# Forming the weights of two neighbouring outputs at once in the second pass of a gated MLP

## The chip, the cores and the metric

The kernel runs on one core of a Trainium2 chip. It is one program that computes the whole network below. The metric is the device time of one execution in microseconds (us); the shown number is the median of several executions. A core has five engines that run their own instruction streams side by side: TensorE (PE in the profile, matrix products into PSUM), VectorE (DVE) and GpSimd (POOL) for elementwise work, ScalarE (ACT) for elementwise functions, and SyncE (SP), which here issues the DMA transfers between device memory and SBUF, the on-chip memory.

## The reference, cut to what matters

Two layers, 1024 tokens of width 1024, float32. Each layer has a mixer (attention in the first, a matrix memory in the second) and then this MLP with D_FF = 2816:

```python
def conv_ffn(h, w_up, conv_w, conv_b, w_down):
    a, g = jnp.split(h @ w_up, 2, axis=-1)
    a = lax.conv_general_dilated(a, conv_w[:, None, :], ...) + conv_b
    return (jax.nn.gelu(a, approximate=False) * g) @ w_down
...
    h = rms_norm(x) * (1 + sc_f) + sh_f
    x = x + g_f * conv_ffn(h, ffn_w_up[i], ffn_conv_w[i], ffn_conv_b[i], ffn_w_down[i])
```

The change touches only the product with w_down (2816 x 1024), once in each layer.

## The kernel before, in words

Activations are held transposed: 128 features on the partitions, 512 tokens (half of the sequence) along the free dimension. Weights come in tiles of 128 input features by 128 output features.

**Three products for one.** A float32 matrix `v` is held as two: `hi`, the ScalarE copy of `v` in the format fp32r, and `lo = v - hi`, the rest, formed by a subtraction on VectorE or GpSimd. `mm3` (L172 to L177) forms one product as `hi*hi`, then `hi` of the weight with `lo` of the activation, then `lo` of the weight with `hi` of the activation. So PE needs the weight's `lo` first at the third matmul of a tile.

**Seven products for eight.** The MLP is a 2x2 block product done with seven block products instead of eight (a Strassen-Winograd scheme). In the second pass the blocks of the weight are: the output tiles p = 0..3 against p + 4 (two rows of blocks), and two halves of the input features (two columns). For one p, A11 and A12 are the blocks of output p, A21 and A22 those of output p + 4. The weights' operands of the seven products are named in the code B11 (A11), B21 (A12), T1 (the sum A21 + A22), B22, T2, T3 (derived from the sum and the blocks by three subtractions in `derive`) and T4 (A22). The 22 tiles of input features are worked on in three groups `DG` of n = 4, 4 and 3 tiles in each half. A group runs its seven products in the order `ORD`, and each product for p = 0, 1, 2, 3: 28 entries of 3n matmuls. Every entry is added to the running x by `gate_x` (L290 to L294, VectorE, reads PSUM) as soon as it is finished.

**How the weights are formed.** For each group and p, `weights` loads two tiles of 128x1024 (L1152): one with A11 and A12, asked for at B11, and one with A21 and A22, asked for at T1. `d_sum` (L1163) forms the sum of 128x512 into half of a `wsum` tile, `derive` (L1171 to L1173) forms the three differences in place, and `wop` (L988, L989) forms `hi` and `lo` into half of a pair of tiles of 128x1024, so that two entries share a pair. In the last group the width is 384 and not 512. The rest `lo` is formed on GpSimd for T3 and T4, and also for B11 and B21 in the groups after the first; on VectorE otherwise.

**The order of the work.** The list `seq` holds all entries of both passes; the loop at the end of `mlp` forms an entry's weights five entries before it runs it (`LOOK`). Hooks of that list load the activations (`q`, L1121) and x (L1222) and form the activations' operands `U` (L1138 to L1140, VectorE and ScalarE, 128x1024 each). All loads go through SP's queue in order. There are four pairs of `hi` and `lo` tiles, five tiles `raw` (A11, A12 and others), four tiles `raw1` (A21, A22) and two `wsum`. A new load waits until its slot is free. The framework arranges each engine's instructions ahead of time by program order, dependencies and its own estimates of cost, so that the order on an engine can differ from the order in the code; on the chip each engine then runs its list strictly in order. Instructions under `tc.high_priority()`, such as `gate_x`, are put ahead.

## Time and profile before

| | |
|---|---|
| median of 3 runs | 2198.36 us (2195.66 to 2200.03) |
| the profiled execution: span from first to last instruction | 2200.1 us (its time outside the span is not shown) |
| PE busy | 2166.5 us, 98% |
| DVE busy | 1693.1 us, 77% |
| ACT busy | 1046.7 us, 48% |
| POOL busy | 178.3 us, 8% |
| mean granted clock of TensorE | 0.994 |
| second pass of the first layer, first and last matmul into the banks da | start at 903.6 us and 1106.4 us |
| second pass of the second layer, last matmul into da | starts at 2188.4 us |

In the profile's rows, a line such as `x<-da,modc,x` says what an instruction writes and from what, by the names in the code: `whi` and `wlo` are a weight's hi and lo, `da` and `db` the second pass's PSUM banks, `U` its activations' operands, `raw` and `wsum` the weights before they are split. A number in brackets at the end of a timeline row is the time that the engine was idle before the instruction, and what ended it. A row with `x2` joins two instructions that follow each other, and its duration is of both together.

### The profile page before, as it was taken

The page shows a single profiled execution, that of the slowest core. Times are in us where ns is not written, and L with a number is a line of the kernel's source. Part 1 is how long each engine was busy: PE and PEld are TensorE (multiplying, and loading weights), DVE is VectorE, ACT ScalarE, POOL GpSimd, SP SyncE. Part 2 cuts the span into 40 slices and gives each one's busy share as a digit, 9 for nine tenths or more (in the row PEclk, how much of TensorE's full clock was granted, in tenths as well). Part 3 has the DMA queues.
Part 4 walks back from the last instruction along what each step waited for, and adds up shares of the span by engine and source line. Part 5 has one row for each costly group of instructions (what it writes and reads, how often), then busy time and mean ns, then how long its engine had stood idle before and what let it go on. Part 6 is the DMA issues. An engine that isn't in the chain of part 4 may idle for free.

```text
span 2200.1 us, 28740 instructions
## 1 busy us (share of the span) xinstructions
PE 2166.5 (98%) x10557; PEld 1818.0 (83%) x10557; DVE 1693.1 (77%) x2769; ACT 1046.7 (48%) x1812; POOL 178.3 (8%) x216
## 2 busy tenths in 40 slices
PE   9999999999999999999999999999999999999998
PEld 7878888787888888877888888988788888887787
DVE  8877878669878777899973655566887777778997
ACT  6465556446544444543453434344554444453335
POOL 0000000000000000042210111010000000002232
PEclk9999999999999999999999999999999999999999
DMA  8512234832444332542132243444143332245122
GB/s 317 152 50 63 92 109 142 285 125 69 157 139 143 123 125 85 204 151 89 53 121 93 62 131 103 132 157 171 64 144 101 111 120 92 79 163 194 50 80 77
DMA packets 105085, 270.50 MB, mean 123 GB/s; under 512 B 12336, under 2 KB 15984, under 8 KB 104944
## 3 DMA queue, kind: packets, MB, share of 16 engines
q1 hardware_dynamic: 104544, 268.28, 36.9%
q8 instruction: 83, 1.36, 0.3%
q14 instruction: 58, 0.48, 0.1%
q10 hardware_dynamic: 400, 0.39, 0.1%
HBM read 221.53 MB, written 44.47 MB: 121 GB/s over the span
## 4 chain that ended last, share of the span: by engine, by line
PE 85%; DVE 9%; DMA 3%; ACT 2%; issue 1%; POOL 0%; SPq 0%; POOLq 0%; DVEq 0%; ACTq 0%
PE pa L175 7%; PE pa L177 7%; PE pa L176 7%; PE pd L177 3%; PE pd L175 3%; PE pd L176 3%; PE sc L673 3%; PE op L175 3%; PE op L176 3%; PE op L177 2%; PE inp L177 2%; PE da L175 2%; PE inp L175 2%; PE inp L176 2%; PE da L176 2%; PE db L175 2%
## 5 line engine op out<-in xcount | busy, mean ns | idle before, releaser
L988 ACT ACTIVATE whi<-raw 128x512 fp32r<-128x512 f32 (+1 forms) x252 | 147.3, 607 | 243.2 <-PE pb L176 61.0
L988 ACT ACTIVATE whi<-wsum 128x512 fp32r<-128x512 f32 (+1 forms) x224 | 134.0, 617 | 181.8 <-PE pa L176 61.5
L175 PE MATMUL pa<-T,whi 128*128 128x512 f32 x528 | 205.9, 390 | 0.0
L176 PE MATMUL pa<-T,whi 128*128 128x512 f32 x528 | 205.4, 389 | 0.0
L177 PE MATMUL pa<-T,wlo 128*128 128x512 f32 x528 | 205.1, 389 | 0.0
L989 DVE TENSOR_TENSOR wlo<-wsum,whi 128x512 fp32r<-128x512 f32 (+1 forms) x224 | 151.1, 690 | 32.8 <-ACT whi L988 31.5
L989 POOL TENSOR_TENSOR wlo<-raw,whi 128x512 fp32r<-128x512 f32 (+1 forms) x80 | 119.9, 1515 | 401.7 <-ACT whi L988 394.0
L175 PE MATMUL da<-U,whi 128*128 128x512 f32 (+1 forms) x364 | 139.5, 383 | 3.4 <-DVE x L294 3.4
L177 PE MATMUL da<-U,wlo 128*128 128x512 f32 (+1 forms) x364 | 138.4, 383 | 2.0 <-DVE wlo L989 2.0
L176 PE MATMUL da<-U,whi 128*128 128x512 f32 (+1 forms) x364 | 139.2, 382 | 0.0
L989 DVE TENSOR_TENSOR wlo<-raw,whi 128x512 fp32r<-128x512 f32 (+1 forms) x172 | 115.7, 679 | 24.9 <-ACT whi L988 24.9
L167 ACT ACTIVATE whi<-wraw 128x1024 fp32r<-128x1024 f32 x67 | 70.7, 1059 | 117.1 <-PE op L176 59.2
L175 PEld LDWEIGHTS pa<-T,whi 128*128 128x128 f32 x528 | 99.1, 188 | 22.2 <-ACT whi L988 1.2
L177 PEld LDWEIGHTS pa<-T,wlo 128*128 128x128 f32 x528 | 99.1, 188 | 20.6
L176 PEld LDWEIGHTS pa<-T,whi 128*128 128x128 f32 x528 | 99.1, 188 | 20.3
L1140 DVE TENSOR_TENSOR U<-q,U 128x1024 fp32r<-128x1024 f32 x84 | 102.9, 1241 | 14.0 <-ACT U L1139 13.6
L1028 ACT ACTIVATE ct<-a,cols 128x512 f32<-128x512 f32 x88 | 70.8, 808 | 83.9 <-DVE a L1050 47.9
L175 PE MATMUL db<-U,whi 128*128 128x512 f32 x264 | 103.3, 391 | 1.3 <-ACT whi L988 1.3
L168 DVE TENSOR_TENSOR wlo<-wraw,whi 128x1024 fp32r<-128x1024 f32 x67 | 81.7, 1222 | 29.4 <-ACT whi L167 27.2
L177 PE MATMUL db<-U,wlo 128*128 128x512 f32 x264 | 102.9, 390 | 0.0
L176 PE MATMUL db<-U,whi 128*128 128x512 f32 x264 | 102.8, 389 | 0.0
L1139 ACT ACTIVATE U<-q 128x1024 fp32r<-128x1024 f32 x84 | 79.7, 979 | 47.7 <-DVE q L1138 22.2
(378 smaller groups left out, 6097.3 us busy)
## 6 DMA issues: line engine op xcount, KB each, us to landing
raw<-in_wf SPq DMA_DIRECT2D x96, 512.0 KB, 4.0
wraw<-in_w SPq DMA_DIRECT2D x67, 512.0 KB, 3.7
mraw<-in_mod_w SPq DMA_DIRECT2D x56, 512.0 KB, 4.0
ud<-ct SPq DMA_DIRECT2D x88, 256.0 KB, 2.4
q<-ud SPq DMA_DIRECT2D x88, 256.0 KB, 4.6
raw<-in_wd SPq DMA_DIRECT2D x32, 512.0 KB, 6.4
pa<-in_mod_w SPq DMA_DIRECT2D x24, 512.0 KB, 3.7
x<-xd SPq DMA_DIRECT2D x48, 256.0 KB, 4.8
```

Of the source, the lines that this page charges most:

```text
L167: act.activation(hi, raw, AF.Copy)
L168: dve.tensor_tensor(lo, raw, hi.bitcast(F32), ALU.subtract)
L175: pe.matmul(ps, lh, rh, start=first, stop=False, skip_group_check=more)
L176: pe.matmul(ps[:, 0:rl.shape[-1]], lh, rl, start=False, stop=False, skip_group_check=more)
L177: pe.matmul(ps, ll, rh, start=False, stop=last, skip_group_check=more)
L673: pe.matmul(ps[:, cs], a[:, qs if n < 3 else qrs_], b[:, cs], start=n == 0, stop=n == 4)
L988: act.activation(hi, src, AF.Copy)
L989: eng.tensor_tensor(lo, src, hi.bitcast(F32), ALU.subtract)
L1028: act.activation(t, a[:, 2:], AF.Identity, bias=col(f"cb{l}", m), scale=cw(m, 2))
L1139: act.activation(hi, w, AF.Copy)
L1140: dve.tensor_tensor(lo, w, hi.bitcast(F32), ALU.subtract)
```

## The change

Everything that `weights`, `d_sum`, `derive` and `d_w` did for one output p is now done for the outputs p and p + 1 together. A load no longer brings two blocks of one output, but one block of two outputs (`block_of`, with b = 0..3 for A11, A12, A21, A22): 512 KB as before, in two runs of 2 KB per partition where there was one of 4 KB. So A11 of a pair is asked for at B11, A12 at B21, and A21 and A22 at T1, each at the even p of the pair. The sum (`two_sum`), the three differences (`derive`) and the split into `hi` and `lo` (`d_two`) work on 128x1024 (128x768 in the last group) and are issued once for a pair, five entries ahead of the even p; the odd p's entry then finds its parts ready. The choice of engine for each rest is the same. Numbers and sizes of the tiles are the same, and so are all matmuls and everything outside the second pass.

```diff
--- before.py
+++ after.py
@@ -1144,44 +1144,56 @@
             for _ in operand(i):
                 pass
 
-        def weights(g, p, i):
+        def block_of(g, p, b):
 
             k0, n = DG[g]
-            if (g, p, i) not in W:
-                t = (pd[0] if i else px).tile([P, 1024], F32, tag=f"raw{i}" if i else "raw", bufs=4 if i else RAWS, name=nm("raw"))
-                nc.sync.dma_start(t[:, 0:2 * n * P], wd[l, p + 4 * i, :, k0 * P:(k0 + 2 * n) * P])
-                W[g, p, i] = t[:, 0:n * P], t[:, n * P:2 * n * P]
-            return W[g, p, i]
-
-        sums = []
-
-        def d_sum(g, p):
-            if not sums:
-                t = wp.tile([P, 1024], F32, tag="wraw", bufs=wraws, name=nm("wsum"))
-                sums.extend(t[:, i * HS:(i + 1) * HS] for i in range(2))
-            W[g, p, "s"] = sums.pop(0)[:, 0:DG[g][1] * P]
-            dve.tensor_tensor(W[g, p, "s"], *weights(g, p, 1), ALU.add)
+            if (g, p, b) not in W:
+                t = (pd[0] if b > 1 else px).tile([P, 1024], F32, tag="raw1" if b > 1 else "raw",
+                                                  bufs=4 if b > 1 else RAWS, name=nm("raw"))
+                c0 = (k0 + b % 2 * n) * P
+                v = t[:, 0:2 * n * P]
+                nc.sync.dma_start(v.rearrange("q (p c) -> q p c", p=2),
+                                  wd[l, p + b // 2 * 4:p + b // 2 * 4 + 2, :, c0:c0 + n * P].rearrange("p q c -> q p c"))
+                W[g, p, b] = v
+            return W[g, p, b]
+
+        def two_sum(g, p):
+
+            W[g, p, "s"] = wp.tile([P, 1024], F32, tag="wraw", bufs=wraws, name=nm("wsum"))[:, 0:2 * DG[g][1] * P]
+            dve.tensor_tensor(W[g, p, "s"], block_of(g, p, 2), block_of(g, p, 3), ALU.add)
             return W[g, p, "s"]
 
         def derive(g, p):
 
             if (g, p, "d") not in W:
                 W[g, p, "d"] = True
-                sm, (a11, a12), (a21, _) = W[g, p, "s"], weights(g, p, 0), weights(g, p, 1)
+                sm, a11, a12, a21 = W[g, p, "s"], *[block_of(g, p, b) for b in range(3)]
                 dve.tensor_tensor(sm, sm, a11, ALU.subtract)
                 dve.tensor_tensor(a11, a11, a21, ALU.subtract)
                 dve.tensor_tensor(a21, a12, sm, ALU.subtract)
 
+        def d_two(g, p, op):
+            if op in ("B11", "B21"):
+                src, eng = block_of(g, p, int(op == "B21")), pool if g else dve
+            elif op == "T1":
+                src, eng = two_sum(g, p), dve
+            elif op == "T4":
+                src, eng = block_of(g, p, 3), pool
+            else:
+                derive(g, p)
+                src = {"B22": block_of(g, p, 2), "T2": W[g, p, "s"], "T3": block_of(g, p, 0)}[op]
+                eng = pool if op == "T3" else dve
+            n = src.shape[-1]
+            hi, lo = [wp.tile([P, 1024], F32R, tag=f"w{j}", bufs=wbufs, name=nm(f"w{j}"))[:, 0:n] for j in ("hi", "lo")]
+            act.activation(hi, src, AF.Copy)
+            eng.tensor_tensor(lo, src, hi.bitcast(F32), ALU.subtract)
+            for i in range(2):
+                W[g, p + i, op] = [x[:, i * n // 2:(i + 1) * n // 2] for x in (hi, lo)]
+
         def d_w(g, p, op):
-            if op in ("B11", "B21"):
-                return wop(weights(g, p, 0)[op == "B21"], pool if g else dve)
-            if op == "T1":
-                return wop(d_sum(g, p), dve)
-            if op == "T4":
-                return wop(weights(g, p, 1)[1], pool)
-            derive(g, p)
-            return wop({"B22": weights(g, p, 1)[0], "T2": W[g, p, "s"], "T3": weights(g, p, 0)[0]}[op],
-                       pool if op == "T3" else dve)
+            if (g, p, op) not in W:
+                d_two(g, p, op)
+            return W[g, p, op]
 
         bank_a, bank_d, stats = {}, {}, {}
 
@@ -1245,11 +1257,7 @@
                         hook(len(seq) - 1, lambda i=i, gen=gen: gen.append(operand(i + 3)))
                     if p in (0, 2) and t0 == 0 and 0 < i and i + 3 < len(order):
                         hook(len(seq) - 1, lambda gen=gen, p=p: piece(gen[0], 1 + p))
-                    if t0 == 0:
-                        make = lambda g=g, p=p, op=op: W.setdefault((g, p, op), None) or W.__setitem__(
-                            (g, p, op), d_w(g, p, op)) or W[g, p, op]
-                    else:
-                        make = lambda g=g, p=p, op=op: W[g, p, op]
+                    make = lambda g=g, p=p, op=op: d_w(g, p, op)
                     seq.append((make, lambda w, i=i, p=p, t0=t0, width=width: d_run(i, p, w, t0, width)))
```

## The prediction

> **What bounds the kernel now.** I read the page's busy shares and chain first, then the engines' shares in the stages of the second pass, then TensorE's waits there one by one, and last what VectorE and GpSimd did just before each wait.
>
> ```profile
> span 2200.1 us, 28740 instructions
> PE 2166.5 (98%) x10557; PEld 1818.0 (83%) x10557; DVE 1693.1 (77%) x2769; ACT 1046.7 (48%) x1812; POOL 178.3 (8%) x216
> ...
> PE 85%; DVE 9%; DMA 3%; ACT 2%; issue 1%; POOL 0%; SPq 0%; POOLq 0%; DVEq 0%; ACTq 0%
> ```
>
> TensorE (PE) is busy for 98% of the span, and the change takes no matmul away. It can only save time in which PE waits inside the MLPs' second passes, so I look for that time. The four stretches below are the first group of each layer's second pass (919 to 960 and 1980 to 2021) and the change from its first to its second group (960 to 1000 and 2021 to 2061).
>
> ```profile
> 919.00:960.00 41.00, 39.36 (x172) 31.74 (x171) 40.42 (x54) 13.69 (x20) 2.98 (x2) 1.00 0.46 171
> 960.00:1000.00 40.00, 38.65 (x170) 31.41 (x169) 34.99 (x33) 17.78 (x25) 23.91 (x14) 1.00 0.36 128
> 1980.00:2021.00 41.00, 39.35 (x172) 31.93 (x172) 40.65 (x53) 13.94 (x21) 2.98 (x2) 1.00 0.45 164
> 2021.00:2061.00 40.00, 37.95 (x165) 30.53 (x165) 34.03 (x32) 17.45 (x24) 24.46 (x14) 1.00 0.37 128
> ```
>
> The columns are PE, weight loads, VectorE (DVE), ScalarE (ACT), GpSimd (POOL), each in us with its count, then the granted clock, the DMA share and GB/s. DVE is full in the first stretch (40.42 of 41) while ACT works a third of it; in the second, POOL works 23.91 of 40. The granted clock is 1.00 throughout. PE's waits there, all of them above 0.15 us:
>
> ```profile
> 951.79 0.50 PE L177 MATMUL da<-U,wlo 128*128 128x512 f32 x1 [1.01 <-DVE wlo L989]
> 955.45 0.50 PE L175 MATMUL db<-U,whi 128*128 128x512 f32 x1 [0.63 <-ACT whi L988]
> 994.21 0.47 PE L175 MATMUL da<-U,whi 128*128 128x512 f32 x1 [0.82 <-DVE x L294]
> 997.74 0.47 PE L175 MATMUL da<-U,whi 128*128 128x512 f32 x1 [0.53 <-DVE x L294]
> 2012.48 0.50 PE L177 MATMUL da<-U,wlo 128*128 128x512 f32 x1 [1.00 <-DVE wlo L989]
> 2016.14 0.50 PE L175 MATMUL db<-U,whi 128*128 128x512 f32 x1 [0.65 <-ACT whi L988]
> 2051.93 0.47 PE L175 MATMUL da<-U,whi 128*128 128x512 f32 x1 [0.56 <-DVE x L294]
> 2055.84 0.47 PE L175 MATMUL da<-U,whi 128*128 128x512 f32 x1 [0.95 <-DVE x L294]
> 2059.38 0.47 PE L175 MATMUL da<-U,whi 128*128 128x512 f32 x1 [0.53 <-DVE x L294]
> ```
>
> In the first layer they add up to 1.01+0.63+0.82+0.53 = 2.99 us, in the second to 1.00+0.65+0.56+0.95+0.53 = 3.69. So **6.7 us is the most that the change can gain** here. They are of two kinds: **place one**, where weights' parts (rests) come late in the first group, and **place two**, where the addition of a finished product to x (L294) comes late as the second group begins. Both are lateness of DVE.
>
> **The change part by part.** The 84 pairs of hi and lo parts of each layer's second pass become 42 pairs of double width; so do 12 sums (6) and 36 derived blocks (18). In group 0, T3 and T4 have their rests on POOL and the other five products on DVE; in groups 1 and 2 it is four on POOL and three on DVE. On DVE that is 20+12+12 rests, 12 sums and 36 derived blocks, or 92 instructions that become 46.
>
> *VectorE.* Two half-width instructions back to back against one of full width:
>
> ```profile
> 928.18 0.69 DVE L1163 TENSOR_TENSOR wsum<-raw 128x512 f32<-128x512 f32 x1 [0.57 <-DMA raw<-in_wd]
> 928.79 1.22 DVE L1138 TENSOR_TENSOR q<-q 128x1024 f32<-128x1024 f32 x1
> 929.92 0.75 DVE L294 SCALAR_TENSOR_TENSOR x<-db,modc,x 128x512 f32<-128x512 f32 x1
> 930.58 1.28 DVE L989 TENSOR_TENSOR wlo<-wsum,whi 128x512 fp32r<-128x512 f32 x2
> ```
>
> Two of 128x512 take 1.28 us together and one of 128x1024 takes 1.22, so a merged pair saves 0.06. The 46 pairs save 2.8 us of DVE a layer, but only those before a wait count. In 926.9 to 951.7 I count 22 such instructions (4 sums, 4+3+1 rests, 10 derived), 11 pairs: 0.7 us before place one, in each layer.
>
> [...]
>
> *GpSimd.* The changed kernel has a 128x1024 rest here, which this trace does not show. The nearest rows:
>
> ```profile
> 960.37 1.29 POOL L989 TENSOR_TENSOR wlo<-raw,whi 128x512 fp32r<-128x512 f32 x1 [9.18 <-ACT whi L988]
> 1055.58 1.02 POOL L989 TENSOR_TENSOR wlo<-raw,whi 128x384 fp32r<-128x384 f32 x1 [2.46 <-ACT whi L988]
> ```
>
> 128 elements more cost 0.27, so 512 cost 1.08 and 0.21 is fixed: a pair takes about 2.37 (an estimate; bounds 2.16 with no fixed part, 2.58 for two whole ones), and 0.21 is saved, within 0 to 0.42. While POOL works, DVE's two-input instructions are slowed:
>
> ```profile
> 985.57 1.66 DVE L1140 TENSOR_TENSOR U<-q,U 128x1024 fp32r<-128x1024 f32 x1
> 987.15 2.31 DVE L1138 TENSOR_TENSOR q<-q,q 128x1024 f32<-128x1024 f32 x1
> 989.38 0.74 DVE L294 SCALAR_TENSOR_TENSOR x<-da,modc,x 128x512 f32<-128x512 f32 x1
> ...
> 982.57 5.80 POOL L989 TENSOR_TENSOR wlo<-raw,whi 128x512 fp32r<-128x512 f32 x3 [2.78 <-PE da L177]
> ```
>
> 1.22 became 2.31, about one POOL instruction more (1.09 of 1.29), and POOL's three took 5.80 and not 3.87; L294, which reads PSUM, kept its 0.74. In 960 to 1000 stand 14 POOL instructions; as 7 pairs they save 7 x 0.21 = 1.5 us of POOL. I take half as given back to DVE (bounds 0 and all): 0.7 a layer, just before place two.
>
> *ScalarE.* One conversion of 128x1024 costs 1.06 for two of 0.61 to 0.62:
>
> ```profile
> L988 ACT ACTIVATE whi<-raw 128x512 fp32r<-128x512 f32 (+1 forms) x252 | 147.3, 607 | 243.2 <-PE pb L176 61.0
> L167 ACT ACTIVATE whi<-wraw 128x1024 fp32r<-128x1024 f32 x67 | 70.7, 1059 | 117.1 <-PE op L176 59.2
> L168 DVE TENSOR_TENSOR wlo<-wraw,whi 128x1024 fp32r<-128x1024 f32 x67 | 81.7, 1222 | 29.4 <-ACT whi L167 27.2
> ```
>
> ACT's own saving I cost at nothing, since ACT idles two thirds of the first stretch; without that cover it would be 42 x 0.15 = 6 us a layer.
>
> *What comes later for the first of a pair.* Its parts now wait for the second: +0.45 us on ACT, +0.54 on DVE (1.22 less 0.68), +1.08 on POOL, and its three derived blocks +1.6. The kernel forms weights five products ahead, and one product is 12 matmuls, 0.23 us apart (below), 2.7 us, so 13.6 us cover this unless DVE's backlog has eaten them, as it has at place one. There the second of the pair comes earlier by nearly as much. I take no net cost, with 0.54 a layer (the rest of T2's second output formed before its first can run) as the upper bound.
>
> *Loads.* Bytes and counts stay: four 512 KB tiles per group and half, now as 256 runs of 2 KB and not 128 of 4 KB. SP's queue is passed by them in another order: A12's blocks are asked for at B21 and no longer at B11, ahead of x's tiles of half 0.
>
> ```profile
> raw<-in_wd SPq DMA_DIRECT2D x32, 512.0 KB, 6.4
> out<-x SPq DMA_DIRECT2D x4, 512.0 KB, 2.8
> 920.53 2.79 SPq L1152 DMA_DIRECT2D raw<-in_wd x4
> 926.92 0.68 DVE L1163 TENSOR_TENSOR wsum<-raw 128x512 f32<-128x512 f32 x1
> 931.03 0.39 PE L175 MATMUL db<-U,whi 128*128 128x512 f32 x1
> 931.26 0.39 PE L176 MATMUL db<-U,whi 128*128 128x512 f32 x1
> ```
>
> The stores to out have that same split form and land in 2.8, in a quiet queue; the loads' 6.4 is queueing. I take the split as free (bounds: 2.8 and 6.4 to land). A12's block goes into a tile slot that was free before, so I expect no delay of x. But T1's **first sum now waits for two blocks**: the second one landed just before 928.18, and the sum would start then and not at 926.92. DVE idles 1.26 there in place of 0.57, so 0.7 are lost in the first layer. Behind it in DVE's order stand a difference of q, an addition to x and the rest, and PE wants that rest at 931.26+0.23 = 931.49. In the second layer the sums start late enough that the second block is nearly there:
>
> ```profile
> 1987.68 1.28 DVE L1163 TENSOR_TENSOR wsum<-raw 128x512 f32<-128x512 f32 x2
> ```
>
> There, I take 0.4 (bounds 0 and 0.7).
>
> *Sum.* Place one: 0.7 saved less 0.7 waited = 0 in the first layer, 0.7-0.4 = 0.3 in the second. Place two: 0.7 in each, and two pairs of sums there, 2 x 0.06 = 0.1 each: 1.6. Together 1.9 us, so the profiled 2200.1 would become 2198.2. This profile's span lies 1.7 above the median of the runs, 2198.36; no time outside the span is shown. From the median: 2198.36-1.9 = **2196.4**. Its own range: nothing saved at place two and 0.54 lost twice is 2198.36-0.3+1.1 = 2199.2, and everything given back (0.7 more a layer) with no wait for blocks 2198.36-1.9-1.4-1.1 = 2194.0.
>
> **The rivals.**
> *A, the waits vanish.* If the order of DVE's work also falls better, since A12's slot comes free when the blocks are derived and not at T3, and the next group's loads start earlier, all 6.7 us go: 2191.7. For it speaks that every wait is under 1.02 us; against it that place two is overload by POOL, whose elements stay.
>
> *B, POOL holds DVE longer (slower).* Place: the additions to x at the change to the second group, and T2's first rest at place one:
>
> ```profile
> 948.21 2.98 POOL L989 TENSOR_TENSOR wlo<-raw,whi 128x512 fp32r<-128x512 f32 x2 [98.17 <-ACT whi L988]
> 948.30 1.74 DVE L1171 TENSOR_TENSOR wsum<-wsum,raw 128x512 f32<-128x512 f32 x1
> 949.96 1.77 DVE L989 TENSOR_TENSOR wlo<-wsum,whi 128x512 fp32r<-128x512 f32 x1
> ```
>
> Two DVE instructions that take 0.68 elsewhere take 1.74 and 1.77 beside two of POOL, and PE's wait at 951.79 follows. If a DVE instruction is held for one whole POOL instruction, it is held 2.37 in place of 1.29, 1.08 more, with an addition to x queued behind it. At each of the seven waits of these kinds (2+5) that is +7.6: 2206.0. It decides as soon as additions to x have less than 1.08 us of room before their bank is wanted again, and at five places they have none. Against it: as many elements pass POOL, so half as many instructions are held.
>
> [...]
>
> *C, the wait for two blocks decides.* The sum starts at 928.18, ends 1.22 later at 929.4; the conversion (1.06) ends at 930.5; with the difference of q (1.13) and the addition (0.67) ahead of it, the rest runs from 931.2 to 932.4, and PE waits 0.9 at 931.49. With 0.4 in the second layer, and nothing gained: 2198.36+1.3 = 2199.7.
>
> *D, it does nothing on the path*, if DVE's order is so fixed by other work that each saved bit becomes idle time: 2198.4.
>
> **How the numbers follow.** The forecast (a gain of up to 4.4) has 0.38, A 0.25, B 0.20, C 0.12, D 0.05. A measurement of this kernel can tell 0.2%, 4.4 us, from no change. Faster than that are A and the forecast's best end (0.09): 0.34. Slower are B and the case that C meets a worse order of work (0.04): 0.24. The rest is 0.42. The range reaches to A with more gained outside the waits, 2189, and to all of B, 2206.
>
> **What would show it.** Right: 42 pairs of parts a layer, DVE's 128x1024 rests at 1.22 and POOL's near 2.4 alone; the waits at place two shorter by half a microsecond a layer, those at place one nearly as before. B shows as DVE instructions of 3.5 us and additions to x that release PE later. C shows as a wait of T1's first product for its rest, and an idle DVE of over 1 us before the first sum. The prediction is wrong if the order of products on PE changes in the second pass, or if a wait appears at B22's third product, whose derived blocks now come in one lump of 3.6 us.

## The result, and the profile after

The changed kernel takes **2211.64 us** (median of 5 runs, 2209.56 to 2212.59), the kernel before 2198.36 (5 runs, 2195.3 to 2200.86). The ratio is 1.0065, with a 95% interval of 1.0054 to 1.0075: the change costs 13.3 us. It was forecast to save 2.

The page of the changed kernel begins as follows; the last line is the chain that ended last.

```profile
span 2209.7 us, 28482 instructions
PE 2169.6 (98%) x10557; PEld 1819.9 (82%) x10557; DVE 1702.4 (77%) x2677; ACT 1037.5 (47%) x1728; POOL 159.7 (7%) x176
...
PE 83%; DVE 10%; DMA 3%; ACT 2%; issue 1%; SPq 1%; POOL 0%; DVEq 0%; POOLq 0%; ACTq 0%
```

The counts are those of the edit: VectorE (DVE) has 92 instructions fewer, ScalarE (ACT) 84 and GpSimd (POOL) 40. POOL is 18.6 us less busy and ACT 9.2. But DVE is **9.3 us busier** with fewer instructions, where 46 merged pairs a layer at 0.06 each should have made it 2 x 46 x 0.06 = 5.5 us less busy. Some 15 us of DVE's time therefore went into instructions that took longer than their work.

The same stretches as in the prediction, by engine (columns: PE, weight loads, DVE, ACT, POOL in us with counts, granted clock, DMA share, GB/s):

```profile
919.00:960.00 41.00, 39.50 (x173) 31.72 (x172) 39.38 (x38) 13.77 (x14) 7.29 (x2) 1.00 0.58 193
960.00:1000.00 40.00, 36.88 (x155) 29.59 (x154) 38.41 (x29) 15.38 (x16) 17.31 (x6) 0.96 0.25 87
1980.00:2021.00 41.00, 39.55 (x173) 31.82 (x172) 39.20 (x38) 13.25 (x13) 7.29 (x2) 1.00 0.60 195
2021.00:2061.00 40.00, 33.91 (x144) 27.01 (x143) 38.22 (x29) 15.02 (x15) 16.59 (x6) 0.98 0.30 96
```

The first stretch of each layer is as before (173 matmuls in both, before 172 in both). The second has lost 15 matmuls in the first layer and 21 in the second, and DVE is fuller there (38.41 and 38.22, before 34.99 and 34.03), with 29 instructions where there were 33 and 32. PE's waits in these places:

```profile
930.88 0.50 PE L177 MATMUL db<-U,wlo 128*128 128x512 f32 x1 [1.10 <-DVE wlo L1189]
947.45 0.50 PE L175 MATMUL db<-U,whi 128*128 128x512 f32 x1 [0.40 <-ACT whi L1188]
980.67 0.79 PE L175 MATMUL da<-U,whi 128*128 128x512 f32 x1 [2.91 <-DVE x L294]
...
1993.16 0.50 PE L177 MATMUL db<-U,wlo 128*128 128x512 f32 x1 [1.05 <-DVE wlo L1189]
2009.75 0.50 PE L175 MATMUL db<-U,whi 128*128 128x512 f32 x1 [0.40 <-ACT whi L1188]
2043.10 0.50 PE L175 MATMUL da<-U,whi 128*128 128x512 f32 x1 [3.04 <-DVE x L294]
2052.55 0.47 PE L175 MATMUL da<-U,whi 128*128 128x512 f32 x1 [0.99 <-ACT whi L1188]
2057.59 0.50 PE L175 MATMUL da<-U,whi 128*128 128x512 f32 x1 [2.06 <-DVE x L294]
...
2176.93 0.38 PE L250 MATMUL st<-ones,ssq 128*128 128x1 f32 x2 [0.47 <-DVE ssq L241]
2178.26 0.40 PE L250 MATMUL st<-ones,sq 128*128 128x1 f32 x2 [0.94 <-ACT sq L229]
```

Place one (the first two and the fourth and fifth row) makes 1.10+0.40+1.05+0.40 = 2.95, before 0.63+1.01+1.00+0.65 = 3.29. Place two, with a small further wait of 0.21 at 996.2, makes 2.91+0.21+3.04+0.99+2.06 = 9.2, before 3.4. The last two rows are new: the sums of squares for the final norm at the end.

After some of these waits TensorE runs at half clock for a while. Three windows of the changed kernel show it in the granted clock, the column behind that of POOL:

```profile
980.00:984.00 4.00, 3.33 (x8) 2.65 (x9) 4.00 (x5) 1.06 (x1) 0.00 (x0) 0.57 0.00 0
2059.00:2063.00 4.00, 4.00 (x13) 3.09 (x12) 4.00 (x5) 1.06 (x1) 0.00 (x0) 0.57 0.00 0
2176.00:2188.00 12.00, 10.59 (x43) 8.73 (x42) 5.17 (x9) 5.79 (x13) 2.82 (x2) 0.72 0.00 0
```

A clock of 0.57 over 4 us is a loss of 0.43 x 4 = 1.7 us, which is half of a stretch of 3.4 us; 0.72 over 12 us is a loss of 0.28 x 12 = 3.4, two such stretches. Together they cost 6.8 us. The kernel before had a clock of 1.00 at the same work, in the second-pass rows of the prediction and at its end:

```profile
2166.00:2178.00 12.00, 12.00 (x64) 10.18 (x64) 7.06 (x12) 8.04 (x17) 4.58 (x5) 1.00 0.00 1
```

The granted clock of the changed kernel is 0.50 from 980.41 to 983.82 us, from 2059.02 to 2062.43 and from 2178.49 to 2185.31: two stretches of 3.41 us, and one of 6.82. The last section has the rows of PE's work ahead of them.

Both kernels have 10557 matmuls in the trace, and they can be matched by number except at one place in each layer, inside the first two groups of the table below. There the order of products on PE has changed: from 950.2 us the kernel before runs 14 matmuls into da, two into db, six into da and ten into db, and the changed kernel from 948.5 us five into da and then twenty into db. T2's first product, which waited for its rest at 951.79 before, now stands mostly behind B22's. Groups that begin and end outside that place hold the same matmuls in both kernels, so the time that they take is the sharpest view of where the 13.3 us lie:

| from matmul to matmul | before | after | |
|---|---|---|---|
| 4391 to 4730 (919 to 1000 us before: first layer, group 0 and the change to group 1) | 81.1 | 84.4 | +3.3 |
| 9597 to 9932 (1980 to 2061 us: the same in the second layer) | 81.0 | 86.7 | +5.7 |
| 10368 to the last (2160 to 2193 us: the end) | 32.8 | 37.5 | +4.7 |
| sum | | | +13.7 |

Outside these three the changed kernel's execution is 4 us faster, by luck of the clock and not by the change. The code there is the same, and the half-clock stretches near 10, 116 and 1350 us last 6.8, 6.8 and 3.4 us in this execution of the kernel before, but 3.4, 3.4 and nothing in that of the changed one, which is 5.1 us of time. So the spans differ by only 9.6 us, while the medians differ by 13.3. The first 40 us of before, and then of after:

```profile
0.00:40.00 40.00, 35.57 (x146) 29.75 (x147) 31.35 (x56) 25.24 (x40) 0.77 (x8) 0.91 0.87 315
```

```profile
0.00:40.00 40.00, 36.08 (x151) 30.29 (x152) 31.25 (x56) 25.73 (x41) 0.77 (x8) 0.96 0.89 319
```

**How the long wait comes about.** VectorE and GpSimd of the changed kernel ahead of PE's wait at 980.67:

```profile
956.51 2.76 DVE L1138 TENSOR_TENSOR q<-q 128x1024 f32<-128x1024 f32 x1
969.86 3.45 DVE L1138 TENSOR_TENSOR q<-q,q 128x1024 f32<-128x1024 f32 x1
973.89 6.06 DVE L1140 TENSOR_TENSOR U<-q,U 128x1024 fp32r<-128x1024 f32 x2
979.88 0.74 DVE L294 SCALAR_TENSOR_TENSOR x<-da,modc,x 128x512 f32<-128x512 f32 x1
```

```profile
955.43 2.76 POOL L1189 TENSOR_TENSOR wlo<-raw,whi 128x1024 fp32r<-128x1024 f32 x1 [0.58 <-DMA q<-ud]
961.39 2.50 POOL L1189 TENSOR_TENSOR wlo<-raw,whi 128x1024 fp32r<-128x1024 f32 x1 [3.20 <-DMA raw<-in_wd]
969.71 2.52 POOL L1189 TENSOR_TENSOR wlo<-raw,whi 128x1024 fp32r<-128x1024 f32 x1 [5.81 <-ACT whi L1188]
```

POOL's first ends at 955.43+2.76 = 958.19. DVE's instruction from 956.51 ends at 959.27, which is 1.08 us later, close to its own 1.22: it gets to its work about when POOL has ended. The same holds at 969.86: POOL ends at 972.23, DVE at 973.31, again 1.08 later. POOL's pair takes 2.50 where it is not held itself (961.39). An instruction of 1.22 us now takes 2.76 to 3.45. The addition to x (L294) keeps its 0.74 as before, but it stands behind two such instructions (6.06 us together), ends at 980.62, and 0.05 later PE starts.

The group rows of 54 us around the change to group 1 in the first layer, of before and then of after, have ten additions to U each:

```profile
L1140 DVE TENSOR_TENSOR U<-q,U 128x1024 fp32r<-128x1024 f32 x10 | 14.9, 1501 | 2.5 <-ACT U L1139 2.5
```

```profile
L1140 DVE TENSOR_TENSOR U<-q,U 128x1024 fp32r<-128x1024 f32 x10 | 18.9, 1896 | 1.7 <-ACT U L1139 1.7
```

Ten of 1.22 would be 12.2. They are held for 2.7 us before and 6.7 after. POOL gains in the same exchange: three rests of 128x512 took 5.80 beside DVE before, so two of them 3.87, and its pair takes 2.76 now. In the second layer's 54 us the additions to U and the differences of q show the same, again before and then after:

```profile
L1140 DVE TENSOR_TENSOR U<-q,U 128x1024 fp32r<-128x1024 f32 x11 | 16.2, 1476 | 3.4 <-ACT U L1139 3.4
L1138 DVE TENSOR_TENSOR q<-q 128x1024 f32<-128x1024 f32 x4 | 4.8, 1213 | 0.0
```

```profile
L1140 DVE TENSOR_TENSOR U<-q,U 128x1024 fp32r<-128x1024 f32 x9 | 16.1, 1801 | 1.8 <-ACT U L1139 1.8
L1138 DVE TENSOR_TENSOR q<-q 128x1024 f32<-128x1024 f32 x6 | 10.4, 1754 | 0.0
```

11 x 1.22 = 13.4, so 2.8 held before; 9 x 1.22 = 11.0 and 6 x 1.22 = 7.3, so 5.1+3.1 = 8.2 after. With all groups that are held (the other differences of q, the sums and the rests too), the held time goes from 9.0 to 13.5 us in the first layer's window and from 9.0 to 14.2 in the second's: 9.7 us more.

### The profile page after: what moved, and what is told of

Read it like the earlier page. It is cut to its first block, busy times and chain, and to the rows that moved or that the text cites. A ratio compares the mean times of both kernels' runs of the same rounds, so it can differ in the third digit from the quotient of the medians.

```text
span 2209.7 us, 28482 instructions
## 1 busy us (share of the span) xinstructions
PE 2169.6 (98%) x10557; PEld 1819.9 (82%) x10557; DVE 1702.4 (77%) x2677; ACT 1037.5 (47%) x1728; POOL 159.7 (7%) x176
## 3 DMA queue, kind: packets, MB, share of 16 engines
q1 hardware_dynamic: 110688, 268.28, 37.5%
## 4 chain that ended last, share of the span: by engine, by line
PE 83%; DVE 10%; DMA 3%; ACT 2%; issue 1%; SPq 1%; POOL 0%; DVEq 0%; POOLq 0%; ACTq 0%
PE pa L175 7%; PE pa L177 7%; PE pa L176 7%; PE sc L673 3%; PE pd L177 3%; PE pd L175 3%; PE pd L176 3%; PE op L175 2%; PE op L176 2%; PE op L177 2%; PE inp L177 2%; PE inp L175 2%; PE inp L176 2%; PE db L177 2%; PE db L175 2%; PE db L176 2%
## 5 line engine op out<-in xcount | busy, mean ns | idle before, releaser
L988 ACT ACTIVATE whi<-wsum 128x512 fp32r<-128x512 f32 x176 | 107.2, 625 | 126.7 <-PE pa L176 61.5
L989 DVE TENSOR_TENSOR wlo<-wsum,whi 128x512 fp32r<-128x512 f32 x176 | 118.3, 687 | 32.5 <-ACT whi L988 31.2
L1189 POOL TENSOR_TENSOR wlo<-raw,whi 128x1024 fp32r<-128x1024 f32 (+1 forms) x40 | 99.9, 2498 | 433.6 <-DVE wlo L1189 204.3
L988 ACT ACTIVATE whi<-raw 128x512 fp32r<-128x512 f32 x132 | 79.8, 624 | 109.0 <-PE pb L176 61.0
L1140 DVE TENSOR_TENSOR U<-q,U 128x1024 fp32r<-128x1024 f32 x84 | 113.9, 1366 | 12.6 <-ACT U L1139 12.5
L1188 ACT ACTIVATE whi<-raw 128x1024 fp32r<-128x1024 f32 (+1 forms) x60 | 59.1, 985 | 121.3 <-PE da L176 55.7
L989 DVE TENSOR_TENSOR wlo<-raw,whi 128x512 fp32r<-128x512 f32 x132 | 89.7, 686 | 24.9 <-ACT whi L988 24.9
L1139 ACT ACTIVATE U<-q 128x1024 fp32r<-128x1024 f32 x84 | 79.3, 978 | 62.9 <-DVE q L1138 27.7
L175 PE MATMUL db<-U,whi 128*128 128x512 f32 x264 | 104.3, 395 | 0.8 <-ACT whi L1188 0.8
```

What stands on the lines that cost most here:

```text
L175: pe.matmul(ps, lh, rh, start=first, stop=False, skip_group_check=more)
L988: act.activation(hi, src, AF.Copy)
L989: eng.tensor_tensor(lo, src, hi.bitcast(F32), ALU.subtract)
L1139: act.activation(hi, w, AF.Copy)
L1140: dve.tensor_tensor(lo, w, hi.bitcast(F32), ALU.subtract)
L1189: eng.tensor_tensor(lo, src, hi.bitcast(F32), ALU.subtract)
```

## The experiments

The theories at the start. **L, the hold**: DVE's two-input instructions are held for a whole POOL instruction, and a pair holds them twice as long (the prediction's B). **The coarse unit**: the parts of the first output wait for those of the second, at T1's first product (the prediction's C), and wherever DVE's backlog has eaten the lead. Later came **O**: that the sums of later pairs are pulled ahead in the order of DVE's work, because tiles for A21 and A22 come free one by one; and, for the last run, **D**, that the delivery of the weights in blocks of two outputs costs the time, against **U**, that the width of the units does.

All medians, each beside the kernel before on the same chip, with the time of the three groups of matmuls above in the profiled execution:

| kernel | median us | before there | difference | ratio, 95% | 4391-4730 | 9597-9932 | 10368-end |
|---|---|---|---|---|---|---|---|
| before | | | | | 81.1 | 81.0 | 32.8 |
| changed kernel | 2211.64 | 2198.36 | +13.3 | 1.0054 to 1.0075 | 84.4 | 86.7 | 37.5 |
| pool_halves | 2205.65 | 2195.78 | +9.9 | 1.0031 to 1.0066 | 85.7 | 82.8 | 33.9 |
| t1_halves | 2215.48 | 2195.78 | +19.7 | 1.0063 to 1.0106 | 89.3 | 87.6 | 35.8 |
| both_halves | 2207.58 | 2195.78 | +11.8 | 1.0034 to 1.0064 | 84.1 | 85.1 | 35.5 |
| pool_pairs_only | 2213.41 | 2195.78 | +17.6 | 1.0063 to 1.0099 | 88.0 | 86.2 | 38.6 |
| loads_only | 2201.39 | 2195.80 | +5.6 | 1.0016 to 1.0036 | 81.9 | 82.7 | 32.5 |
| raw1_joint | 2207.87 | 2195.80 | +12.1 | 1.0045 to 1.0079 | 84.0 | 82.6 | 35.8 |
| own_entry | 2201.27 | 2195.80 | +5.5 | 1.0008 to 1.0078 | 83.2 | 82.2 | 33.0 |
| no_pool_rests | 2194.22 | 2195.80 | -1.6 | 0.998 to 0.9999 | 79.3 | 78.4 | 33.3 |
| before_no_pool | 2190.66 | 2196.08 | -5.4 | 0.9965 to 0.9984 | 77.7 | 76.1 | 32.4 |
| all_dve | 2192.71 | 2196.08 | -3.4 | 0.9974 to 0.9993 | 79.5 | 77.8 | 32.5 |
| before_dve | 2189.76 | 2196.08 | -6.3 | 0.9963 to 0.9983 | 77.3 | 76.1 | 32.6 |
| loads_dve | 2191.28 | 2195.71 | -4.4 | 0.9972 to 0.999 | 77.7 | 76.2 | 32.7 |

### POOL's rests in halves (pool_halves)

The changed kernel, with each POOL rest as two instructions of 128x512.

```diff
-            eng.tensor_tensor(lo, src, hi.bitcast(F32), ALU.subtract)
+            parts = 2 if eng is pool else 1
+            for i in range(parts):
+                c = slice(i * n // parts, (i + 1) * n // parts)
+                eng.tensor_tensor(lo[:, c], src[:, c], hi[:, c].bitcast(F32), ALU.subtract)
```

> The changed kernel, with GpSimd's rests formed by two instructions of half width (128x512, one for each output) in place of one of 128x1024; all else stays in pairs. Theory L (a two-input VectorE instruction is held for a whole GpSimd instruction, 2.5 to 2.8 us now and 1.3 before, and the addition to x is queued behind it): the waits for x as the second group begins, 3.1 us in the first layer and 6.1 in the second, fall back to about 1.4 and 2.0 as before the change, and the two stretches at a granted clock near 0.5 that follow them go too (1.6 us each): 2203 us, 8 to 9 under the changed kernel's 2211.6. Rival O (the new order of loads and work on the engines is the cause, not the length of one instruction): within 2 us of 2211.6, the waits for x stay over 2.5 us.

It costs 9.9 us and not 13.3. The first row is PE's total wait for additions to x, in us, times and the longest; the others are the 54 us around the change of group in each layer:

```profile
PE da L175 <- DVE x L294: 8.5, 6, 1.9
```

```profile
948.00:1002.00 54.00, 49.85 (x209) 39.96 (x210) 50.19 (x43) 20.96 (x21) 33.72 (x16) 0.97 0.40 133
2010.80:2064.80 54.00, 49.69 (x216) 39.90 (x215) 49.83 (x42) 20.29 (x22) 33.80 (x16) 1.00 0.39 132
```

The longest wait went from 3.0 to 1.9, but their sum, 8.5, is no smaller than the changed kernel's 8.2: there are six where there were four. What went are three of the four half-clock stretches (the one left is in the first layer, 0.97), 5.1 us, and a part of the waits at the end (the granted clock is 1.00 from 2172 to 2184 us, and the last group of matmuls takes 33.9 and not 37.5). L was right in the direction and in the length of the single hold, and wrong in that the waits would shrink: 3.4 us came back where 8 to 9 were expected. Yet the time for which DVE is held, by the reckoning above, did fall in these windows, to 10.4 and 10.2 us, where the changed kernel has 13.5 and 14.2 and the kernel before 9.0 and 9.0. So the length of the hold is at most a part of what makes DVE late. POOL is at work for 33.7 of the 54 us, against 24.6 with pairs: its halves stand back to back, 5.8 for three, so while one ends the next takes its place. DVE also stands idle longer for ScalarE's hi of U, 3.8 and 4.0 us where the changed kernel has 1.7 and 1.8. Why DVE is as late as with pairs is not settled.

### T1's unit in halves, and both (t1_halves, both_halves)

The changed kernel, where T1's blocks, sum and parts are formed by output; both_halves has the edit of pool_halves too.

```diff
...
-            dve.tensor_tensor(W[g, p, "s"], block_of(g, p, 2), block_of(g, p, 3), ALU.add)
...
+            for i in range(2):
+                c = slice(i * w, (i + 1) * w)
+                for b, v in ((0, a21), (1, a22)):
+                    c0 = (k0 + b * n) * P
+                    nc.sync.dma_start(v[:, c], wd[l, p + 4 + i, :, c0:c0 + w])
+                dve.tensor_tensor(s[:, c], a21[:, c], a22[:, c], ALU.add)
...
+            parts = 2 if op == "T1" else 1
+            for i in range(parts):
+                c = slice(i * n // parts, (i + 1) * n // parts)
+                act.activation(hi[:, c], src[:, c], AF.Copy)
+                if eng is dve:
+                    eng.tensor_tensor(lo[:, c], src[:, c], hi[:, c].bitcast(F32), ALU.subtract)
...
```

> The changed kernel, with T1 alone formed by output again: A21 and A22 are loaded in halves of 256 KB, the first output's two first, and sum, hi and lo are of 128x512. Theory D (the first sum waits for both 512 KB blocks, and T1's first product for its rest): the waits of 1.10 and 1.05 us for that rest go, 2209.5 us, unless the time comes back at the second group (then 2211.6 and waits for x that are longer by as much). Rival (VectorE's backlog and not the load makes the rest late): those waits stay over 0.8 us.

> Both edits: GpSimd's rests and all of T1 in halves; the pairs of VectorE and ScalarE for the other products, the sums' differences and the loads by block stay. If L and D are the whole cause: 2199 to 2202 us, no wait for x over 1 us, granted clock 1.00 throughout the second passes. If the lumps of the remaining pairs matter by themselves (theory U): over 2205.

T1's wait fell from 1.10 and 1.05 to 0.63 and none, as the coarse unit says. But another came in its place, and t1_halves is slower than either of the times that were expected (2215.48; its profiled execution, at 2219.46, is the slowest of its four). A row of t1_halves from its timeline, and its totals:

```profile
952.01 0.80 PE L175 MATMUL db<-U,whi 128*128 128x512 f32 x1 [3.45 <-ACT whi L1200]
```

```profile
PE db L175 <- ACT whi L1200: 6.9, 2, 3.5
PE da L175 <- DVE x L294: 4.5, 3, 2.1
```

This is B22 of the second pair, once in each layer. Behind the row's wait PE's products start 0.43 apart, where they start 0.23 apart ahead of it, and the mean granted clock of this execution is 0.989, in the kernel before 0.994. The three differences of that pair are 3.6 us of DVE's time, but not one lump: in the first layer they start at 943.79, 946.72 and 949.65, with a subtraction for U, one of q and additions to x between them, and the last ends at 950.87; in the changed kernel it ends at 946.26. So T1's first product was only one of several points at which DVE is late. both_halves has no wait for x in the change of group at all, yet the same waits at B22, 6.9 us in two, and still two of 0.72 and 0.87 for rests in the second layer. At 2207.58 it lies where theory U, that the remaining pairs cost time by themselves, had put it (over 2205).

B22's differences by pairs, which the prediction had only as a sign that it was wrong, can thus be a second price of the pairing. In the changed kernel the wait for B22's hi is 0.40. Why DVE's order puts the last difference so much later in these kernels is not shown.

### Only POOL in pairs (pool_pairs_only)

The changed kernel with DVE's and ACT's parts in halves of 128x512 and POOL's rests whole.

```diff
-            act.activation(hi, src, AF.Copy)
-            eng.tensor_tensor(lo, src, hi.bitcast(F32), ALU.subtract)
+            for i in range(2):
+                c = slice(i * n // 2, (i + 1) * n // 2)
+                act.activation(hi[:, c], src[:, c], AF.Copy)
+                if eng is dve:
+                    eng.tensor_tensor(lo[:, c], src[:, c], hi[:, c].bitcast(F32), ALU.subtract)
+            if eng is pool:
+                eng.tensor_tensor(lo, src, hi.bitcast(F32), ALU.subtract)
```

> The other way round: GpSimd's rests stay whole (128x1024), while VectorE's rests and ScalarE's conversions are two instructions of half width each; sums and differences stay whole. Theory L: the waits for x stay over 2.5 us and the time within 3 us of the changed kernel's 2211.6. Theory U (double-width instructions on VectorE and ScalarE delay what is queued behind them): 2203 or less.

It costs 17.6 us, not less than the changed kernel. PE's waits, in total:

```profile
PE db L175 <- ACT whi L1190: 6.6, 2, 3.5
PE da L175 <- DVE x L294: 5.9, 5, 2.1
```

Against both_halves, at 11.8, the waits for x are back (5.9 against none in the change of group). T1's blocks and sum and the other parts of DVE and ACT differ between the two as well, so this is not a measure of the hold alone. It does show that halving DVE's and ACT's instructions where they stand saves nothing.

### Only the blocks (loads_only)

The kernel before, with loads of one block for two outputs; the sums, differences and parts are by output, as before.

```diff
         def weights(g, p, i):
...
+            q, r = p // 2 * 2, p % 2
+            out = []
+            for b in (2 * i, 2 * i + 1) if i else (0, 1):
+                out.append(block_of(g, q, b)[:, r * n * P:(r + 1) * n * P])
+            return out
...
-                return wop(weights(g, p, 0)[op == "B21"], pool if g else dve)
+                q, c = p // 2 * 2, p % 2 * DG[g][1] * P
+                return wop(block_of(g, q, int(op == "B21"))[:, c:c + DG[g][1] * P], pool if g else dve)
```

> The kernel before, with the changed kernel's loads alone: one load brings one block of two outputs, asked for at B11, B21 and T1; sums, differences, conversions and rests stay by output, 128x512, each at its own entry. Theory O (the tiles come free earlier and the next group's work is pulled ahead, or the first sum waits for two blocks): 2203 us or more, with waits for x of over 3 us in all. Theory L or U (it is the width of the instructions): 2194 to 2200, as before the change.

It costs 5.6 us, between what the two theories asked for (2200 or less, 2203 or more). The waits for x are as in the kernel before (3.3, there 3.4), and the mean granted clock of the execution is 0.996, there 0.994. New is one wait at T1's rest, in the second layer, where the prediction had put 0.4:

```profile
1993.11 0.50 PE L177 MATMUL db<-U,wlo 128*128 128x512 f32 x1 [1.54 <-DVE wlo L989]
```

That is 1.5 of the 5.6; the groups of matmuls show +0.8 and +1.7 against the profiled execution of before. The rest I can't place. The interval (1.0016 to 1.0036) is clear of 1, so with POOL at work the blocks cost time by themselves, with no instruction wider than before.

### A21 and A22 in one tile (raw1_joint)

The changed kernel, with one tile of 128x2048 (two of them) for both blocks, so that both come free together.

```diff
-                t = (pd[0] if b > 1 else px).tile([P, 1024], F32, tag="raw1" if b > 1 else "raw",
-                                                  bufs=4 if b > 1 else RAWS, name=nm("raw"))
+                if b > 1 and (g, p, "j") not in W:
+                    W[g, p, "j"] = pd[0].tile([P, 2048], F32, tag="raw1", bufs=2, name=nm("raw"))
+                t = W[g, p, "j"][:, (b - 2) * 1024:(b - 1) * 1024] if b > 1 else px.tile(
+                    [P, 1024], F32, tag="raw", bufs=RAWS, name=nm("raw"))
```

> The changed kernel with A21 and A22 of a pair in one tile of 128x2048 (two tiles in place of four), so that both come free together, at T4, as before the change. Theory O for the sums (the second group's sums are formed some 18 us earlier than before, in the stretch where VectorE has no room): the waits for x fall by half or more and the time to 2206 or less. Rival: within 2 us of 2211.6.

```profile
PE da L175 <- DVE x L294: 6.6, 4, 2.8
```

The cost is 12.1 us in place of 13.3, and the intervals overlap. There are as many waits for x, the longest 2.8 and not 3.0, and 6.6 us in all and not 8.2, where O asked for half. O is not the main cause.

### Every part at its own entry (own_entry)

The changed kernel, with hi and lo by output at that output's own entry; the blocks, sums and differences stay in pairs.

```diff
...
-            act.activation(hi, src, AF.Copy)
-            eng.tensor_tensor(lo, src, hi.bitcast(F32), ALU.subtract)
...
+            return src, eng
...
+                src, eng = W[g, q, op, "src"]
+                W[g, p, op] = wop(src[:, p % 2 * w:(p % 2 + 1) * w], eng)
```

> The changed kernel with hi and lo formed by output again, 128x512, each at its own entry; loads by block, and sums and differences of 128x1024 stay. Theory U for the parts (the double-width conversions and rests are the cause): 2200 or less. If sums and differences in pairs, or the loads, are the cause: over 2205.

It costs 5.5 us (1.0008 to 1.0078, a wide interval, because one of its eight executions took 2232.86), between the 2200 and the 2205 that were expected. There is no wait for x, though POOL does as many rests of 128x512 as in pool_halves; there the two of a pair follow each other directly, here each stands at its own entry. The edit takes DVE's and ACT's parts out of pairs too, so it does not tell which of the three matters. What is left is the wait at B22: PE's wait, and the last of the three differences on DVE.

```profile
949.93 0.50 PE L175 MATMUL db<-U,whi 128*128 128x512 f32 x1 [3.52 <-ACT whi L988]
```

```profile
947.95 1.21 DVE L1173 TENSOR_TENSOR raw<-raw,wsum 128x1024 f32<-128x1024 f32 x1
```

B22's weight is the last of the three differences; it is there at 949.16, the conversion starts at 949.24, and PE starts at 949.93. The first two start at 942.09 and 945.02; other work of DVE stands between them here too.

### POOL's rests left out (no_pool_rests, before_no_pool)

Both kernels, with the rests that POOL forms left out, hi standing in for lo (below, the edit of the changed kernel, which also takes no lo tile for these rests; in the kernel before, `wop` returns hi for both). Neither kernel's output is the reference's.

```diff
...
-            eng.tensor_tensor(lo, src, hi.bitcast(F32), ALU.subtract)
+            if eng is pool:
+                lo = hi
+            else:
+                eng.tensor_tensor(lo, src, hi.bitcast(F32), ALU.subtract)
```

> The changed kernel with GpSimd's rests left out: T3, T4, B11 and B21 (the last two after the first group) use hi in the place of the rest, so the output is not the reference's. Theory L in a wider form (what GpSimd's instructions hold on VectorE, 13 us per layer as the second group begins, makes the additions to x late): no wait for x over 0.3 us there, no drop of the granted clock behind it, about 2201 us. Rival (VectorE's own backlog of wide instructions in its new order): waits for x of over 2 us in all stay.

> The kernel before, with GpSimd's rests left out in the same way (T3, T4, and later B11 and B21, use hi in the place of the rest; the output is not the reference's). Theory L: the waits for x at the second group (1.35 and 2.04 us) go, 2191 to 2193 us. Against the changed kernel without those rests (2194.2) it tells what pairing does when GpSimd holds nothing: the theory that only the holding makes pairing lose expects the two within 2 us of each other; the rival, that pairing also loses by VectorE's lumps, expects this one 4 us or more lower.

In the changed kernel all waits for x go. The granted clock is 1.00 in the 54 us around both changes of group, and the last group of matmuls takes 33.3 us and not 37.5. It is faster than the 2201 that was expected. The 54 us around the first change of group, and what is left of PE's waits:

```profile
949.40:1003.40 54.00, 54.00 (x238) 44.48 (x239) 49.34 (x51) 24.12 (x24) 0.00 (x0) 1.00 0.41 141
```

```profile
PE db L177 <- DVE wlo L1193: 2.2, 2, 1.1
```

PE is busy for all 54.00 us. Against their own runs of before, the two kernels stand at -1.6 and -5.4. So POOL's rests cost the changed kernel 13.3+1.6 = **14.9 us** and the kernel before **5.4**, which is 9.5 less. The other 5.4-1.6 = **3.8** of the 13.3 come with the pairing even where POOL holds nobody; the two theories had asked for under 2 and for 4 or more. This is the split of the result by POOL's work. Each of the three differences is known to about 2 us either way.

### All rests on VectorE (all_dve, before_dve, loads_dve)

The rests that POOL forms are formed by DVE: in the changed kernel (the diff), likewise in the kernel before, and in loads_only.

```diff
-                src, eng = block_of(g, p, int(op == "B21")), pool if g else dve
+                src, eng = block_of(g, p, int(op == "B21")), dve
...
-                src, eng = block_of(g, p, 3), pool
+                src, eng = block_of(g, p, 3), dve
...
-                eng = pool if op == "T3" else dve
+                eng = dve
```

> The changed kernel with the rests of GpSimd formed by VectorE, still in pairs of 128x1024 (GpSimd idle in the second pass). Theory L: as the second group begins, eight of GpSimd's rests hold VectorE for 13.3 and 14.1 us, and formed by VectorE itself they take 8 x 1.13 = 9.0: the waits for x shrink, 2197 to 2204 us, no VectorE instruction of 128x1024 over 1.4 us. Rival (VectorE has no room for more): slower than the changed kernel's 2211.6.

> The same edit on the kernel before: all rests by VectorE, 128x512. There GpSimd's fourteen hold VectorE for 7.5 us in each layer's stretch and would take it 14 x 0.60 = 8.4: within 3 us of before, 2194 to 2199. If it is 3 us or more faster, the holding costs more than the held time that the rows show; if all_dve beats it, pairing gains once GpSimd is out of the way.

> The kernel before with the loads by block alone, and all rests by VectorE, 128x512 (so that GpSimd holds nothing). It splits the 2.95 us between all_dve (2192.71) and before_dve (2189.76). Theory D (the first sum waits for both blocks): a wait of T1's first product for its rest of 0.5 to 1.5 us in one or both layers and 2191 to 2193. Theory U (the double width of sums, differences and parts makes T1's and B22's parts late): no such wait, 2189 to 2190.5.

All three are faster than both kernels, the first two by more than was expected. **before_dve, the kernel before with its rests on DVE alone, is the fastest**: 2189.76 against 2196.08, a ratio of 0.9973 (0.9963 to 0.9983). The stretches around the first change of group, of before, of after, of all_dve and of before_dve:

```profile
949.60:1003.60 54.00, 51.02 (x222) 40.96 (x221) 48.99 (x50) 23.47 (x32) 25.49 (x15) 1.00 0.41 146
```

```profile
947.70:1001.70 54.00, 50.88 (x215) 40.88 (x215) 52.35 (x41) 20.75 (x21) 24.60 (x8) 0.97 0.40 133
```

```profile
947.70:1001.70 54.00, 53.77 (x237) 44.30 (x238) 52.85 (x56) 24.41 (x25) 0.00 (x0) 1.00 0.40 134
```

```profile
948.30:1002.30 54.00, 54.00 (x239) 44.60 (x238) 53.13 (x71) 23.13 (x32) 0.00 (x0) 1.00 0.42 148
```

With POOL's work added, DVE does 71 instructions in 53.13 us, where before it did 50 in 48.99. In the changed kernel 52.35 us are full with 41. DVE's busy time here is therefore no measure of its work. PE has no wait at either place in before_dve.

all_dve and before_dve differ by 2.95 us, the price of the pairing with no hold, beside the 3.8 from the kernels without POOL's rests. POOL's work, moved and not left out, is worth 13.3+3.4 = 16.7 us to the changed kernel and 6.3 to the kernel before, 10.4 apart, beside the 9.5. PE's waits that all_dve has left in the second passes add up to 1.10+0.40+0.18+0.78+0.40 = 2.9. loads_dve was to tell D from U. It has the loads' shape alone, and one wait:

```profile
930.92 0.50 PE L177 MATMUL db<-U,wlo 128*128 128x512 f32 x1 [0.30 <-DVE wlo L989]
```

Its median lies between the two, with intervals that overlap both. D asked for a wait of 0.5 or more; the groups of matmuls put only 0.4+0.1 = 0.5 us on the loads and (79.5-77.7)+(77.8-76.2) = 3.4 on the units. The medians put 1.9 on the loads. How the 2.95 are divided stays open, with the profile on the side of U.

## Why the prediction was wrong, by its steps

**What held.** PE's waits at the places named were the thing that moved, in the kinds that were named: T1's rest, B22's hi, additions to x. ScalarE's saving (9.2 us of busy time) was put at nothing, and no run tests it apart. The pairs' single duration on DVE is 1.22 where nothing holds it, and POOL's pair is 2.50 where nothing holds it, against an estimate of 2.37 with an upper bound of 2.58. Place one was forecast to change little, and went from 3.29 to 2.95, though not as the steps had it. One of the prediction's own signs of being wrong came, the changed order of products on PE. The order alone is not the price: all_dve has it too and is faster than the kernel before.

**The step that failed is the POOL term**: "0.21 is saved" for a pair, and "half as given back to DVE: 0.7 a layer". Where nothing holds POOL, a pair takes 2.50 in place of 2 x 1.29, so 0.08 is saved. Its busy time fell by more, 18.6 over 40 pairs, as it is held less by DVE: a rest of 128x512 took 1.73 on average before, and a pair 2.88 after. But nothing was given back to DVE, and the term has the wrong sign: DVE is held for 4.5 and 5.2 us more in the two windows, and place two went from 3.4 to 9.2 us of waits. The prediction had written beside it the row that decides, a DVE instruction held for 1.09 by a POOL instruction of 1.29, and rival B made of it the mechanism that the rows above show. What weighed against B was "as many elements pass POOL, so half as many instructions are held". The group rows show that this doesn't even out: ten additions to U are held for 6.7 us and not for 2.7. The rows at 956.51 and 969.86 show the hold for POOL instructions of 2.76 and 2.52 as well: in both, DVE ends 1.08 after POOL. No row of the kernel before could show that.

**Rival B had the mechanism, but its price is not confirmed.** It gave 7 x 1.08 = 7.6 for holds that are each longer. Taking that length away again (pool_halves) gives back 3.4; all that POOL's rests do costs 9.5 more in the changed kernel than before. B's 2206.0 is nearer to the result than the forecast, but its price is neither of these two. It also spread the price evenly over seven waits, with place one among them. Place one did not grow; place two and the end of the kernel took it all.

**A cost that no case had: the clock.** Waits under 1.02 us left the clock at 1.00 before. In the changed kernel there are four half-clock stretches of 3.4 us, worth 6.8 us, which is half of the result. They come with POOL's rests: with these left out (no_pool_rests) or on DVE (all_dve), the granted clock is 1.00 around both changes of group, and the last group of matmuls takes 33.3 and 32.5 us. With them priced, B would have ended above 2206, and the range would have had to reach further.

**The end of the kernel was not looked at.** The last operands of U are formed beside POOL too (2.08 for an addition to U at 2159.11), and ACT has a conversion of double width (0.83) in front of the squares that the last sums wait for:

```profile
2162.43 0.83 ACT L1188 ACTIVATE whi<-raw 128x768 fp32r<-128x768 f32 x1
```

The last 188 matmuls took 4.7 us longer, of which half clock is 3.4. The conversion alone is not it: no_pool_rests and all_dve form it at double width too, with no rest formed on POOL, and their ends take 33.3 and 32.5 us, as before (32.8). What POOL's rests do there is not followed further.

**The two-block wait** (C) came as its mechanism has it. DVE idles 1.53 before the first sum (forecast 1.26):

```profile
926.67 1.23 DVE L1163 TENSOR_TENSOR wsum<-raw,raw 128x1024 f32<-128x1024 f32 x1 [1.53 <-DMA raw<-in_wd]
```

T1's rest is late by 1.10 and 1.05, where C had 0.9 and 0.4. The forecast's 0.7 and 0.4 were short of it, and in the second layer the second block was not "nearly there". The blocks are not the whole of it: with T1 formed by output 0.63 is left in the first layer. T2's rest is not late any more, now that most of its first product stands behind B22's, and B22's hi is late by 0.40 in place of 0.63.

**"No net cost" for the parts that come later** holds for place one and not beyond. With POOL's rests on DVE the pairing costs 2.95 us, and of PE's waits that are left there (2.9 us) 1.9 are at T1's rest and 1.0 at conversions, near the upper bound of 2 x 0.54 = 1.1. In the changed kernel the wait of 0.99 for a conversion at 2052.55, in place two, is new. And in the four kernels where T1's or DVE's other parts are formed in halves (t1_halves, both_halves, pool_pairs_only, own_entry) PE waits for B22 once in each layer (6.6 to 6.9 us in two waits, the longest 3.5). Its cover, a lead of 13.6 us, is what DVE's backlog had eaten, and the prediction said so only for place one.

**What the parts add up to, and what stays open.** By POOL's work, the 13.3 us are 9.5 of what POOL's rests cost more and 3.8 of the pairing without them. The 9.5 are not all the price of longer holds. The 9.7 us by which DVE is held longer in the two windows agree with them by chance: in pool_halves 7.1 of the 9.7 are gone, and only 3.4 us come back. Taking the pairing back piece by piece gives another split: 3.4 for POOL's wide instructions (13.3 to 9.9), 4.4 for parts that are formed in pairs (9.9 to own_entry's 5.5), and 5.5 for the blocks with their sums and differences, of which loads_only alone has 5.6. With POOL's rests on DVE, the blocks cost 1.9 by the medians. So what is shown is that POOL's rests turn a pairing of some 3 us into one of 13.3. That they do it by holding DVE is argued from the rows, where additions to x stand behind held instructions. Why DVE is as late with holds of the old length (an order of work set without knowing of the holds is the likely reason) is not shown.

## What to carry to other kernels

Where an instruction of one engine holds one of another until it ends, as POOL's rests did DVE's differences of q and additions to U here, joining two instructions of the holder makes the longest holds about twice as long (here from 1.1 to 2.2 us), and the other engine's urgent work waits behind them. Fewer instructions were no gain here, and the work was cheaper on the engine that is held (before_dve, 2189.76 us against 2196.08), even though that one is the fuller of the two (77% of the span, POOL 8%). Ask of a merged unit what stands first in line for its first half, at every place where the lead is used up, and not only at the first. And a wait on TensorE that can grow to about 2 us should be priced with a chance of a half-clock stretch behind it, here 1.7 us each.

## What was not expected of the hardware

- The hold is not shared out fairly by width: beside DVE, two of POOL's rests of 128x512 took 3.87 (of the three in 5.80) and its one of 128x1024 took 2.50 to 3.01 from 955 to 979 us, while DVE's 1.22, which had become 2.31 beside the rests of 128x512, became 2.76 to 3.45. Over all of them, two rests of 128x512 took 2 x 1.73 = 3.46 and one of 128x1024 took 2.88. The wider instruction gained here, and the other engine lost.
- A wait did not bring half clock by its length alone here; where it fell mattered. The half-clock stretches at 980.41 and 2059.02 us are 3.413 us long in the trace, and their starts lie at whole multiples of that from each other: 980.41 and 2059.02 lie 316 of them apart, 2059.02 and 2178.49 lie 35. Counted on that grid, the wait of 3.04 us that ends at 2043.10 is cut in two by a boundary near 2041.96: PE is idle for 1.89 us of the step ahead of it and 1.14 of the step behind, and neither brings half clock; those of 2.91 and 2.06 leave PE idle for 2.65 and 1.98 us within one step of the grid, and the next step runs at half clock. Three such steps follow. The granted clock in a row, 1.00, is that of the step itself; after the first and the third the next step runs at half clock:

```profile
977.00:980.41 3.41, 0.76 (x4) 0.30 (x2) 3.41 (x2) 0.00 (x0) 1.87 (x1) 1.00 0.01 2
2038.54:2041.96 3.42, 1.53 (x7) 0.94 (x5) 3.42 (x2) 0.69 (x1) 2.76 (x1) 1.00 0.00 0
2055.61:2059.02 3.41, 1.43 (x6) 1.21 (x7) 3.41 (x4) 0.00 (x0) 0.18 (x1) 1.00 0.00 0
```

Between 903 and 1106 us and between 1960 and 2160 us of the profiled executions of the kernel before and of the changed one, the first and the third of these steps, with 2.65 and 1.98 us of idle PE, are the only ones that half clock follows; no other step at full clock has more than 1.89. That is what these two traces show; no run tries it for other matmuls. The stretch at the end follows a step with 1.41 us of idle PE only (2175.08 to 2178.49), among matmuls of one column; why it comes so early is not shown.
- DVE's additions to x, which read PSUM and one operand elsewhere, took 0.74 beside POOL's wide instructions (the one at 955.85) as they do alone (the one at 979.88).
